# Two transformer blocks on one Trainium2 core: all tile arithmetic taken off GpSimd, three streams into one PSUM sum in the first block, the modulation GEMV at other places of the weight stream

## Chip, core and metric

The kernel runs on one core of a Trainium2 chip. The metric is the device time of one execution in microseconds (us). Engines are named as in the profile: PE (TensorE, matmuls), PEld (its weight loads), DVE (VectorE), ACT (ScalarE), POOL (GpSimd), SP (the queue that issues every DMA here).

## What is computed

One sequence of 256 tokens, width 2048, passes two different blocks, in float32. Cut to its products:

```python
h = rmsnorm(x, mix_norm_w)
u, qkv, z, b_raw, a_raw, g_s5, g_dn = split(h @ w_in)
y_s5 = gelu(s5_scan(u) + d * u)                        # complex diagonal state space
glu_a, glu_b = split(y_s5 @ s5_glu_w)
y_dn = deltanet(silu(causal_conv4(qkv)), z, b_raw, a_raw)   # 8 heads, chunked delta rule
merged = sigmoid(g_s5) * (glu_a * sigmoid(glu_b)) + sigmoid(g_dn) * (y_dn @ dn_proj_w)
x = x + merged @ w_out
act, val = split(causal_conv3(rmsnorm(x, ffn_norm_w) @ ffn_up))
x = rmsnorm(x + (silu(act) * val) @ ffn_down, final_norm_w)
# block 2
sh1, sc1, g1, sh2, sc2, g2 = split(silu(c) @ w_mod + b_mod)     # the GEMV, 2048 x 12288
h = rmsnorm(x) * (1 + sc1) + sh1
y = merge(window_attention(h @ w_in_2), gated_linear_attention(h @ w_in_2)) @ w_out_2
x = x + g1 * rmsnorm(y)
h = rmsnorm(x) * (1 + sc2) + sh2
x = x + g2 * rmsnorm((silu(gate) * val) @ w_down_2),  gate, val = split(causal_conv3(h @ w_up_2) + b)
```

## The kernel before

**The weight stream.** All weights, some 600 MB, pass once through the core. They are cut into jobs, one for each product (`job_list`): block 1 has u, ba, q, k, v, z, gs, glu, gdn, dnp, wout, up1a, dw1a, up1b, dw1b; block 2 has qa, ka, va, gk, qb, kb, vb, og, ga, gb, wba, wbb, wout2, up2a, dw2a, up2b, dw2b. A job is a list of groups of 128-column tiles. A chunk of up to 1 MB is fetched by one DMA (`fetch`, three buffers `raw`). `split` cuts a unit of 1024 columns of it into a high part `hi` (ACT, L413, a cast to fp32r) and the rest `lo` = raw - hi (L271, on DVE, or on POOL for the units that `on_pool` names). Activations are kept in the same two parts, 256 columns each, side by side in 512 columns.

**The product** (`run`). In form F, for every tile of k and every column tile, the loaded weights `hi` meet the 512 columns of both activation parts, and `lo` meets the 256 columns of the high part:

```python
T.matmul(cur[:, f, :], hi[:, s], x, start=first, stop=False)                    # L451
T.matmul(cur[:, f, 0:L], lo[:, s], x[:, 0:L], start=False, stop=last)           # L452
```

So one half of the PSUM bank holds hi*hi + lo*hi and the other hi*lo; `halves` adds them (an ACT copy, L469, and a DVE addition, L271, into a tile `ev`). In form T (wout, dw, va, vb: L457 to L459) the weights are what streams, and three matmuls of the same width go into one sum. Below, "a step" is one pair of tiles: a pair of matmuls in form F, three in form T.

**Evacuations** (`ev_u`, `ev_qkv`, `ev_z`, `ev_gate`, `ev_glu`, `ev_dnp`, `ev_up` and those of block 2) are generators, moved one yield at each few steps. In block 1 most multiply `ev` by the token scale `R` on POOL. `ev_gate` turns tanh into a gate on POOL and spills it to DRAM, whence `ev_glu` and `ev_dnp` load it.

**Beside the stream** run two background generators in block 1: `s5_task` (in eight rounds of `tables`, products, scans; `cmul` once ahead) and, after it, `dn_task`; in block 2 `attention_task` and `gla_task`. Their POOL operations go through `tt` (L271) and `ts` (L275) with the engine as the last argument. The sums of squares for the first norm are made on POOL from x.

**The GEMV.** `plan` puts 96 chunks of `w_mod` into the stream, one 1 MB transfer each, by the table `MOD_EVERY` (every second or third chunk of the jobs named). `split` multiplies and sums each on DVE (L404). `modulation` reads the results: 32 of the 96 at the start of block 2, the last 48 at its FFN.

What sets the order: each engine works its queue in order; the Tile scheduler makes the queues from the program order. Everything, transfers included, is issued by SP in one queue.

Of the kernel before, what the change touches and what calls it, by code (L numbers as in the profile page):

```python
# [256 lines left out]
class Kern:  # L257
# [131 lines left out]
    def on_pool(self, u):
        """Whether GpSimd makes the low parts of a unit."""  # L390
        j = self.chunks[self.units[u][0]][0].name
        n = u - self.job_start[j]
        e = self.POOL_EVERY.get(j, 0)
        return j in ("qa", "up2a") and n < 4 or e and n % e == 1
# [1507 lines left out]
```

## Time and profile before

| what | value |
|---|---|
| device time, median of 3 runs | 3260.02 us (3258.59 to 3263.13) |
| span of the profiled execution, first to last instruction | 3257.4 us |
| PE busy, share of the span | 3099.1 us, 95% |
| DVE busy | 2300.3 us, 71% |
| ACT busy | 1589.3 us, 49% |
| POOL busy | 872.4 us, 27% |
| HBM traffic over the span | 214 GB/s |
| mean granted PE clock | 0.985 |

The profiled execution's own time is known by its span alone; the median of the runs lies 2.6 us above that. Matmuls overlap in the records, so PE counts as busy even where it has slack; how densely it is fed is seen by the distance from one matmul to the next, or by the number of matmuls in a stretch.

### The profile page before, as it was taken

To read this page: it belongs to the slowest core of one execution; us is meant where nothing else is said; L and a number is where in the kernel's file an instruction comes from. 1 tells how busy PE (TensorE), PEld (TensorE's weight loads), DVE (VectorE), ACT (ScalarE), POOL (GpSimd) and SP (SyncE) were. 2 spreads that over 40 slices of the span, in tenths; PEclk is the share of its full clock that TensorE was granted. 3 is DMA by queue.
4 is the path that set the end of the run, shared out by engine and by line. 5 is a ranking of instruction groups with operands and counts; after the bars stand their busy time and mean duration, and the time that the engine had idled before them with its cause. 6 is when DMAs were issued, how large, how long until landed. Compare 5 with 4: busy or idle time off the path is not lost.

```text
span 3257.4 us, 46596 instructions
## 1 busy us (share of the span) xinstructions
PE 3099.1 (95%) x18220; PEld 2665.1 (82%) x18220; DVE 2300.3 (71%) x3043; ACT 1589.3 (49%) x2276; POOL 872.4 (27%) x491
## 2 busy tenths in 40 slices
PE   7889999999988999989989999999997999999998
PEld 6767789888877788777878898778887888898887
DVE  8999775666777767777667767887566666456655
ACT  4445543554444434444444544645444655445543
POOL 3665452231355403554020000332211111001101
PEclk9999999999999999999999999999998999999999
DMA  6334464665566677666756668666755555555553
GB/s 242 132 127 141 174 227 156 237 235 207 220 240 244 236 264 263 254 245 241 256 188 241 228 247 317 240 248 247 278 194 184 206 192 184 187 198 186 190 192 131
DMA packets 130829, 701.73 MB, mean 215 GB/s; under 512 B 20200, under 2 KB 33176, under 8 KB 53680
## 3 DMA queue, kind: packets, MB, share of 16 engines
q1 hardware_dynamic: 130608, 698.75, 60.0%
q8 instruction: 143, 2.34, 0.3%
q14 instruction: 78, 0.64, 0.1%
HBM read 674.26 MB, written 24.44 MB: 214 GB/s over the span
## 4 chain that ended last, share of the span: by engine, by line
PE 44%; DVE 3%; DMA 1%; issue 1%; ACT 1%; DVEq 0%; SPq 0%; ACTq 0%
PE main L451 19%; PE main L452 10%; PE main L457 5%; PE main L458 5%; PE main L459 5%; DMA raw<-in_wmod 1%; DVE lo L271 1%; DVE X L271 0%; PE bank L634 0%; DVE big L278 0%; ACT L282 0%; DVE raw L404 0%; DVE asm L275 0%; ACT X L282 0%; PE bank L1663 0%
## 5 line engine op out<-in xcount | busy, mean ns | idle before, releaser
L451 PE MATMUL main<-xs,hi 128*128 128x512 f32 x5440 | 1922.5, 396 | 17.2 <-ACT hi L413 9.2
L271 DVE TENSOR_TENSOR lo<-raw,hi 128x1024 fp32r<-128x1024 f32 x940 | 1201.3, 1282 | 628.7 <-ACT hi L413 626.1
L452 PE MATMUL main<-xs,lo 128*128 128x256 f32 x5440 | 1541.4, 284 | 56.4 <-DVE lo L271 38.7
L413 ACT CAST hi<-raw 128x1024 fp32r<-128x1024 f32 (+1 forms) x1024 | 1063.2, 1043 | 1000.7 <-PE main L451 560.5
L451 PEld LDWEIGHTS main<-xs,hi 128*128 128x128 f32 x5440 | 1030.5, 190 | 250.3 <-DVE xs L278 10.7
L452 PEld LDWEIGHTS main<-xs,lo 128*128 128x128 f32 x5440 | 1031.5, 190 | 83.6 <-DVE lo L271 49.8
L271 POOL TENSOR_TENSOR tmp<-tmp 128x256 f32<-128x256 f32 (+1 forms) x93 | 187.6, 2017 | 647.0 <-ACT tmp L282 646.6
L271 POOL TENSOR_TENSOR lo<-raw,hi 128x1024 fp32r<-128x1024 f32 x84 | 211.5, 2518 | 534.3 <-ACT hi L413 447.5
L404 DVE CUSTOM_DVE_ANT_0 raw<-raw,sc 128x2048 f32<-128x2048 f32 x96 | 242.4, 2525 | 42.2 <-DMA raw<-in_wmod 41.7
L271 POOL TENSOR_TENSOR ev<-ev,R 128x512 f32<-128x512 f32 x76 | 140.4, 1847 | 282.6 <-DVE ev L271 282.6
L278 DVE SCALAR_TENSOR_TENSOR tmp<-ev,pv,tmp 128x255 f32<-128x255 f32 (+1 forms) x352 | 162.7, 524 | 74.7 <-ACT tmp L282 74.7
L282 ACT ACTIVATE tmp<-ev,pv 128x256 f32<-128x256 f32 x176 | 88.1, 548 | 119.5 <-POOL ev L271 119.3
L271 DVE TENSOR_TENSOR ev<-main,evlo 128x512 f32<-128x512 f32 (+1 forms) x190 | 129.0, 679 | 14.3 <-ACT evlo L469 10.5
L457 PE MATMUL main<-hi,xs 128*128 128x256 f32 (+1 forms) x448 | 138.6, 309 | 0.0
L458 PE MATMUL main<-lo,xs 128*128 128x256 f32 (+1 forms) x448 | 137.4, 307 | 0.0
L459 PE MATMUL main<-hi,xs 128*128 128x256 f32 (+1 forms) x448 | 137.1, 306 | 0.0
L469 ACT COPY evlo<-main 128x512 f32<-128x512 f32 (+1 forms) x203 | 117.0, 576 | 13.7 <-PE main L452 13.7
L271 POOL TENSOR_TENSOR ev<-ev,tmp 128x512 f32<-128x512 f32 (+1 forms) x48 | 59.4, 1238 | 200.1 <-DVE ev L271 107.0
L451 PE MATMUL main<-ysp,hi 128*128 128x512 f32 x256 | 92.0, 400 | 0.4 <-DVE ev L271 0.4
L457 PEld LDWEIGHTS main<-hi,xs 128*128 128x128 f32 x448 | 84.1, 188 | 6.0 <-issue 1.7
L458 PEld LDWEIGHTS main<-lo,xs 128*128 128x128 f32 x448 | 84.3, 188 | 4.9 <-issue 0.7
L459 PEld LDWEIGHTS main<-hi,xs 128*128 128x128 f32 x448 | 84.5, 189 | 4.7
(336 smaller groups left out, 3863.0 us busy)
## 6 DMA issues: line engine op xcount, KB each, us to landing
raw<-in_w_in SPq DMA_DIRECT2D x164, 1024.0 KB, 4.9
raw<-in_wmod SPq DMA_DIRECT2D x96, 1024.0 KB, 5.1
raw<-in_ffn_up SPq DMA_DIRECT2D x88, 1024.0 KB, 5.0
raw<-in_w_up SPq DMA_DIRECT2D x88, 1024.0 KB, 4.8
raw<-in_ffn_down SPq DMA_DIRECT2D x38, 1024.0 KB, 5.0
raw<-in_w_down SPq DMA_DIRECT2D x38, 1024.0 KB, 4.8
raw<-in_w_out SPq DMA_DIRECT2D x32, 1024.0 KB, 4.8
raw<-in_s_glu_w SPq DMA_DIRECT2D x16, 1024.0 KB, 4.9
```

Of the source, the lines that this page charges most:

```text
L271: (eng or self.V).tensor_tensor(out=out, in0=a, in1=b, op=op)
L278: self.V.scalar_tensor_tensor(out=out, in0=a, scalar=s, in1=b, op0=op0, op1=op1)
L282: self.S.activation(out, a, f, bias=bias, scale=scale, **kw)
L404: self.V.tensor_tensor_reduce(r, r, self.sc, 1.0, 0.0, A.mult, A.add, self.mod[:, m:m + 1])
L413: self.S.copy(hi, r)
L451: T.matmul(cur[:, f, :], hi[:, s], x, start=first, stop=False)
L452: T.matmul(cur[:, f, 0:L], lo[:, s], x[:, 0:L], start=False, stop=last)
L457: T.matmul(cur[:, h, :w], xh, hi[:, s], start=first, stop=False)
L458: T.matmul(cur[:, h, :w], xh, lo[:, s], start=False, stop=False)
L459: T.matmul(cur[:, h, :w], xl, hi[:, s], start=False, stop=last)
L469: self.S.copy(lo[:, :nf], ps[:, :nf, L:])
```

## The change

- **One sum** (`ONE_SUM`, `run`): in the form F jobs of block 1, from u to dnp, and up1a, up1b, the pair of matmuls becomes three of 256 columns into one 256-column sum.
- **Evacuation straight out of PSUM** (`normed`): for these jobs one DVE product of PSUM and `R` stands for copy, addition and POOL product. `ev_glu` and `ev_dnp` read PSUM in a `scalar_tensor_tensor`; the +1 of the gates is folded into it, in block 2 too, and the gates' POOL step is gone.
- **No tile arithmetic on POOL**: `on_pool` is removed (all `lo` on DVE), and the POOL operations of the S5, DeltaNet, attention, GLA, FFN and norm code become DVE operations of the same size. The squares of the first norm are made by ACT from a second copy of x (`xt`, 2 MB, a new transfer at the start) in the buffer `ysp`.
- **The GEMV moved**: 34 of its 96 transfers leave up1a and up1b (20 and 22 there, now 4 and 4) for wout (5), dw1a and dw1b (8 each, now 12), gb (6, now 8), wba (4), wbb (8) and wout2 (7). `modulation` for the FFN of block 2 is read after wout2.
- Comments and docstrings are removed.

```diff
-    MOD_EVERY = {"up1a": 2, "dw1a": 3, "up1b": 2, "dw1b": 3, "qb": 2, "kb": 2, "vb": 2, "og": 2, "ga": 2, "gb": 2, "wba": 2, "wbb": 2}
+    MOD_EVERY = {"wout": 2, "up1a": 11, "dw1a": 2, "up1b": 11, "dw1b": 2, "qb": 2, "kb": 2, "vb": 2, "og": 2, "ga": 2, "gb": 2, "wba": 2, "wbb": 2, "wout2": 2}
...
-                if (ci >= 4 or nm != "up1a") and mods < 96 and since >= self.MOD_EVERY.get(nm, 1 << 30):
+                if (ci >= 6 or nm != "wout") and mods < 96 and since >= self.MOD_EVERY.get(nm, 1 << 30):
...
-    POOL_EVERY = {"gs": 4, "glu": 4, "ga": 4, "gb": 4, "up1a": 4, "up1b": 4}
...
-            eng = self.G if self.on_pool(u) else self.V
-            self.tt(lo, r, hi.bitcast(F32), A.subtract, eng)
+            self.tt(lo, r, hi.bitcast(F32), A.subtract)
...
+    ONE_SUM = ("u", "ba", "q", "k", "v", "z", "gs", "glu", "gdn", "dnp", "up1a", "up1b")
...
+                            if name in self.ONE_SUM:
+                                T.matmul(cur[:, f, 0:L], hi[:, s], x[:, 0:L], start=first, stop=False)
+                                T.matmul(cur[:, f, 0:L], hi[:, s], x[:, L:], start=False, stop=False)
+                                T.matmul(cur[:, f, 0:L], lo[:, s], x[:, 0:L], start=False, stop=last)
+                                continue
...
+    def normed(self, ps, nf=2):
+
+        out = self.sbt([P, 2, L], F32, "ev", 3, "ev")
+        self.tt(out[:, :nf], ps[:, :nf, :L], self.rbc(nf), A.mult)
+        return out
...
-        for i in range(4):
-            self.tt(sq[:, i > 0], x[:, 4 * i:4 * i + 4], x[:, 4 * i:4 * i + 4], A.mult, G)
...
+        xt = self.ys32.rearrange("p (h n) -> p h n", h=2)
+        self.dma(xt, ap["xt"])
+        for h in range(2):
+            self.act(self.tmp[:, 0:2048], xt[:, h], AF.Square, accum=self.ss[0][:, h, 0:1])
...
     def ev_qkv(self, t, ps):
-        raw = self.halves(ps)
-        yield
-        self.tt(raw, raw, self.rbc(2), A.mult, self.G)
-        yield
+        raw = self.normed(ps)
         yield
...
-            self.tt(o, x, p, A.mult, G)
+            self.tt(o, x, p, A.mult)
             self.tt(t3, y, q, A.mult)
...
-            self.roundn(r, e, eng=G)
-            self.tt(e, e, r, A.subtract, G)
-            yield
+            self.roundn(r, e)
+            self.tt(e, e, r, A.subtract)
...
-            self.tt(t1, t1, t2, A.add, G)
-            self.tt(t3, t3, t4, A.subtract, G)
+            self.tt(t1, t1, t2, A.add)
+            self.tt(t3, t3, t4, A.subtract)
...
     def ev_up(self, b, f, i, act, done, ps):
-        raw = self.halves(ps)
-        yield
-        if b == "1":
-            self.tt(raw, raw, self.rbc(2), A.mult, self.G)
-            yield
-            yield
+        raw = self.normed(ps) if b == "1" else self.halves(ps)
+        yield
...
-        self.tt(cv[:, 0], cv[:, 0], cv[:, 1], A.mult, self.G)
+        self.tt(cv[:, 0], cv[:, 0], cv[:, 1], A.mult)
...
-                if h and i in (1, 2):
-                    self.ts(y, y, r1[:, 1:2], A.mult, 0.0, A.add, G)
-                    self.tt(x, x, y, A.add, G)
-                else:
-                    self.stt(x, y, r1[:, h:h + 1], x, A.mult, A.add)
+                self.stt(x, y, r1[:, h:h + 1], x, A.mult, A.add)
...
     def ev_wbb(self, g, ps):
...
-        self.tt(raw, raw, t[:, 0], A.mult, self.G)
-        yield
-        self.tt(self.merged[:, 2 * g:2 * g + 2], raw, t[:, 1], A.add, self.G)
+        self.stt(raw, t[:, 0], 1.0, raw, A.add, A.mult)
+        yield
+        self.tt(self.merged[:, 2 * g:2 * g + 2], raw, t[:, 1], A.add)
```

Where the change moves instructions, three places of the queues show it. First SP at the very start, before and then with the change (`c_71` is a table of constants, `small`, `ysp` and `tmp` take what the S5 task loads):

```order
L285 DMA c_71<-in_c 128x272 [waits DMAHW3_49]
L285 DMA small<-in_s5p 128x96 [waits DMAHW4_49]
L285 DMA ysp<-in_s5c 128x2048 [waits DMAHW5_49]
L285 DMA raw<-in_w_in 128x2048 [waits DMAHW6_49,DVE_49]
L285 DMA raw<-in_w_in 128x2048 [waits DMAHW7_49,DMAHW0_49,DVE_49]
```

```order
L285 DMA c_71<-in_c 128x272 [waits DMAHW3_49]
L285 DMA ysp<-in_xt 128x4096 [waits DMAHW4_49]
L285 DMA small<-in_s5p 128x96 [waits DMAHW5_49]
L285 DMA raw<-in_w_in 128x2048 [waits DMAHW6_49,DVE_49]
L285 DMA raw<-in_w_in 128x2048 [waits DMAHW7_49,DMAHW0_49,DVE_49]
L285 DMA raw<-in_w_in 128x2048 [waits DMAHW2_49,DVE_49]
L285 DMA ysp<-in_s5c 128x2048 [waits DMAHW4_49,DMAHW1_49,Activation_49]
```

The 2 MB of `xt` come ahead of the fourth weight chunk, and the S5 loads now wait for ACT, which squares `xt` in the same buffer.

Second DVE in a round of the S5 task, before and then with the change (`big` holds the task's tables and states, `bank_64` and `bank_65` its PSUM, `pc` a ramp):

```order
L275 TENSOR_SCALAR big<-pc,small 128x128 x4
L271 TENSOR_TENSOR lo<-raw,hi 128x1024
L271 TENSOR_TENSOR ev<-main,evlo 128x512
L271 TENSOR_TENSOR big<-bank_64,big 128x2x128 x2
L271 TENSOR_TENSOR lo<-raw,hi 128x1024
L271 TENSOR_TENSOR big<-bank_65,big 128x2x128 x2
```

```order
L275 TENSOR_SCALAR big<-pc,small 128x128 x4
L1015 SCALAR_TENSOR_TENSOR big<-small,big 128x128 x4
L278 SCALAR_TENSOR_TENSOR big<-ev,pv,big 128x253 x2
L271 TENSOR_TENSOR ev<-main,R 128x512
L271 TENSOR_TENSOR lo<-raw,hi 128x1024
L271 TENSOR_TENSOR big<-big 128x512
L275 TENSOR_SCALAR big<-big 128x512
L271 TENSOR_TENSOR lo<-raw,hi 128x1024
L278 SCALAR_TENSOR_TENSOR big<-big 128x512
```

The 512-wide roundings, differences and sums that stood on POOL now stand between the `lo` of the stream; the evacuation is one row, with `R`, as before.

Third SP in wbb, before and then with the change (`d_gb` and `d_m` are spilled gates and sums, loaded into `tmp`; the numbers are the tensors'):

```order
L285 DMA tmp<-d_m_13725 128x512
L285 DMA raw<-in_w_branch_gla 128x2048 x2
L285 DMA tmp<-d_gb 128x512
L285 DMA tmp<-d_m_13725 128x512
L285 DMA raw<-in_w_branch_gla 128x2048 x2
```

```order
L285 DMA raw<-in_w_branch_gla 128x2048 x2
L285 DMA raw<-in_wmod 128x2048
L285 DMA tmp<-d_gb 128x512
L285 DMA tmp<-d_m_16277 128x512
L285 DMA raw<-in_w_branch_gla 128x2048 x2
L285 DMA raw<-in_wmod 128x2048
L285 DMA tmp<-d_gb 128x512
```

A 1 MB transfer of the GEMV now follows every two of weights there.

## Rows read from the trace of the kernel before

**Rows 1.** The page: the span, and busy time of each engine.
```profile
span 3257.4 us, 46596 instructions
...
PE 3099.1 (95%) x18220; PEld 2665.1 (82%) x18220; DVE 2300.3 (71%) x3043; ACT 1589.3 (49%) x2276; POOL 872.4 (27%) x491
```

**Rows 2.** Windows: stretch, length, busy us (instructions), clock, DMA share, GB/s: gdn, va.
```profile
core 0: us, PE busy (x) PEld busy (x) DVE busy (x) ACT busy (x) POOL busy (x), PEclk, DMA share, GB/s
609.00:697.70 88.70, 88.70 (x514) 78.09 (x513) 48.99 (x49) 44.60 (x56) 17.17 (x16) 1.00 0.62 221
1715.20:1726.70 11.50, 11.50 (x98) 11.50 (x98) 7.62 (x7) 4.69 (x5) 0.00 (x0) 1.00 0.77 271
```

**Rows 3.** Windows again: u to z; gs and glu; up1a; up1b.
```profile
7.40:353.80 346.40, 308.81 (x2153) 247.42 (x2154) 323.55 (x566) 165.25 (x221) 183.32 (x93) 0.95 0.44 157
353.80:609.00 255.20, 246.43 (x1549) 214.60 (x1548) 175.83 (x260) 122.54 (x189) 94.49 (x74) 0.99 0.60 203
835.60:1113.60 278.00, 253.31 (x1418) 215.58 (x1417) 216.35 (x248) 130.22 (x194) 150.84 (x62) 1.00 0.65 242
1241.60:1513.30 271.70, 251.60 (x1410) 215.78 (x1409) 211.44 (x236) 129.89 (x188) 139.93 (x62) 0.99 0.69 251
```

**Rows 4.** Timeline at the start, DVE and POOL: start, us, what.
```profile
13.22 3.21 POOL L271 TENSOR_TENSOR tmp<-tmp 128x1024 f32<-128x1024 f32 x1
...
14.15 9.14 DVE L278 SCALAR_TENSOR_TENSOR xs<-big,pv,xs 128x256 fp32r<-128x256 f32 x4
...
30.01 1.66 DVE L278 SCALAR_TENSOR_TENSOR xs<-big,pv,xs 128x256 fp32r<-128x256 f32 x4
```

**Rows 5.** DVE groups by shape, 7.4 to 373 us: busy us, mean ns, idle before.
```profile
L271 DVE TENSOR_TENSOR lo<-raw,hi 128x1024 fp32r<-128x1024 f32 x87 | 120.7, 1394 | 15.8 <-ACT hi L413 15.7
...
L278 DVE SCALAR_TENSOR_TENSOR big<-ev,pv,big 128x255 f32<-128x255 f32 x24 | 25.9, 1111 | 0.4 <-ACT big L282 0.4
...
L271 DVE TENSOR_TENSOR big<-big 128x512 f32<-128x512 f32 x24 | 15.9, 672 | 0.0
...
L278 DVE SCALAR_TENSOR_TENSOR xs<-big,pv,xs 128x256 fp32r<-128x256 f32 x14 | 15.4, 1153 | 0.6 <-ACT xs L282 0.6
...
L271 DVE TENSOR_TENSOR tmp<-ysp,small 128x1024 f32<-128x1024 f32 x2 | 2.4, 1210 | 0.0
```

**Rows 6.** DVE groups by shape in up2b, 2875.1 to 3119.2 us.
```profile
L271 DVE TENSOR_TENSOR lo<-raw,hi 128x1024 fp32r<-128x1024 f32 x89 | 109.1, 1226 | 59.5 <-ACT hi L413 58.9
L278 DVE SCALAR_TENSOR_TENSOR tmp<-ev,pv,tmp 128x255 f32<-128x255 f32 x42 | 18.3, 477 | 0.0
```

**Rows 7.** POOL groups by shape over the whole span: the S5 rounds.
```profile
L271 POOL TENSOR_TENSOR big<-big 128x512 f32<-128x512 f32 x32 | 51.8, 1635 | 22.7 <-DVE big L271 21.8
...
L275 POOL TENSOR_SCALAR big<-big 128x512 f32<-128x512 f32 x16 | 40.6, 2537 | 36.4 <-DVE big L278 19.5 <-DVE big L275 16.3 <-ACT ev L282 0.7
```

**Rows 8.** Windows: up2a; og; ga and gb; wba; wbb.
```profile
2504.00:2751.60 247.60, 247.60 (x1431) 218.13 (x1430) 171.28 (x243) 146.32 (x214) 30.14 (x21) 1.00 0.55 194
1944.80:2033.60 88.80, 88.80 (x515) 78.19 (x514) 65.56 (x64) 41.22 (x47) 2.42 (x1) 1.00 0.83 309
2033.60:2259.30 225.70, 213.39 (x1218) 181.62 (x1217) 183.10 (x268) 126.41 (x197) 72.65 (x46) 0.98 0.67 236
2259.30:2304.60 45.30, 45.30 (x259) 39.33 (x258) 28.34 (x30) 21.66 (x27) 10.31 (x8) 1.00 0.88 331
2304.60:2393.40 88.80, 88.80 (x515) 78.20 (x514) 50.52 (x51) 42.09 (x54) 24.89 (x15) 1.00 0.71 242
```

**Rows 9.** DVE groups by shape: the GEMV's product in up1a, then in og.
```profile
L404 DVE CUSTOM_DVE_ANT_0 raw<-raw,sc 128x2048 f32<-128x2048 f32 x21 | 59.0, 2808 | 0.8 <-DMA raw<-in_wmod 0.4
...
L404 DVE CUSTOM_DVE_ANT_0 raw<-raw,sc 128x2048 f32<-128x2048 f32 x8 | 18.3, 2289 | 0.7 <-DMA raw<-in_wmod 0.6
```

**Rows 10.** Timeline after wout2: the same four small DVE rows twice.
```profile
2485.53 2.82 DVE L275 TENSOR_SCALAR sm<-sm 128x2 f32<-128x2 f32 x4
...
2498.20 0.64 DVE L275 TENSOR_SCALAR sm<-sm 128x2 f32<-128x2 f32 x4
```

**Rows 11.** PE groups by shape, 7.4 to 373 us: two matmuls of the S5 rounds.
```profile
L1053 PE MATMUL bank<-big,ysp 128*32 128x127 f32 x256 | 13.0, 290 | 11.8 <-DVE big L271 10.2 <-DVE big L278 1.5
...
L1056 PE MATMUL bank<-big,ysp 128*32 128x128 f32 x256 | 8.5, 273 | 0.0
```

More of the change, by code (lines that the diff above doesn't have):

```diff
@@ L385, in fetch @@
             self.dma_at += 1
-    POOL_EVERY = {"gs": 4, "glu": 4, "ga": 4, "gb": 4, "up1a": 4, "up1b": 4}
[L389 to L394, printed above, removed]
     def split(self, upto):
@@ L709, in block1 @@
         self.run("z", self.xrhs, self.ev_z)
-        self.run("gs", self.xrhs, lambda g, ps: self.ev_gate(self.d_gs, g, ps, 1.0))
+        self.run("gs", self.xrhs, lambda g, ps: self.ev_gate(self.d_gs, g, ps))
         while not self.s5_done:
@@ L714, in block1 @@
         self.run("glu", lambda k: self.ysp[:, k], self.ev_glu)
-        self.run("gdn", self.xrhs, lambda g, ps: self.ev_gate(self.d_gdn, g, ps, 2.0))
+        self.run("gdn", self.xrhs, lambda g, ps: self.ev_gate(self.d_gdn, g, ps))
         self.finish(mix, "dn")
@@ L784, in ev_z @@
     def ev_z(self, g, ps):
[L785 to L788 removed]
+        raw = self.normed(ps)
         yield
@@ L794, in ev_z, with ev_gate @@
         self.z_done += 1
-    def ev_gate(self, dst, g, ps, c):
-        raw = self.halves(ps)
-        yield
-        self.tt(raw, raw, self.rbc(2), A.mult, self.G)
-        yield
+    def ev_gate(self, dst, g, ps):
+        raw = self.normed(ps)
         yield
         self.act(raw, raw, AF.Tanh, scale=0.5)
-        yield
-        self.ts(raw, raw, c, A.mult, c, A.add, self.G)
-        yield
         yield
@@ L811, in ev_glu @@
         self.dma(gl, self.d_gs[f // 2][:, L * (f % 2):L * (f % 2) + L])
-        raw = self.halves(ps)
+        raw = self.sbt([P, 2, L], F32, "ev", 3, "ev")
+        self.act(raw[:, 1], ps[:, 1, :L], AF.Tanh, scale=0.5)
         yield
-        self.act(raw[:, 1], raw[:, 1], AF.Tanh, scale=0.5)
+        self.stt(raw[:, 0], raw[:, 1], 1.0, ps[:, 0, :L], A.add, A.mult)
         yield
-        self.stt(raw[:, 0], raw[:, 1], 1.0, raw[:, 0], A.add, A.mult)
-        yield
-        self.tt(raw[:, 0], raw[:, 0], gl, A.mult, self.G)
+        self.stt(raw[:, 0], gl, 1.0, raw[:, 0], A.add, A.mult)
         yield
@@ L833, in ev_dnp @@
         t = self.ml.pop(g)
-        raw = self.halves(ps)
+        raw = self.sbt([P, 2, L], F32, "ev", 3, "ev")
+        self.stt(raw, t[:, 0], 1.0, ps[:, :, :L], A.add, A.mult)
         yield
-        self.tt(raw, raw, t[:, 0], A.mult, self.G)
-        yield
-        self.tt(raw, raw, t[:, 1], A.add, self.G)
-        yield
+        self.stt(raw, raw, 2.0, t[:, 1], A.mult, A.add)
         yield
@@ L1164, in dn_task @@
             ends = lambda t: t.rearrange("p (b n) -> p b n", n=P)[:, 0:3:2]
-            self.tt(k[:, h], k[:, h], r[:, 768:1024], A.mult, G)
-            self.tt(q[:, h], q[:, h], r[:, 1024:1280], A.mult, G)
-            self.tt(ends(at), ends(r[:, 0:384]), tri.unsqueeze(1).to_broadcast([P, 2, P]), A.add, G)
+            self.tt(k[:, h], k[:, h], r[:, 768:1024], A.mult)
+            self.tt(q[:, h], q[:, h], r[:, 1024:1280], A.mult)
+            self.tt(ends(at), ends(r[:, 0:384]), tri.unsqueeze(1).to_broadcast([P, 2, P]), A.add)
             yield
@@ L1374, in ev_down @@
                 self.square_sums(y, self.ss[1][:, :, g], True)
-            self.tt(x, x, row, A.mult, self.G)
+            self.tt(x, x, row, A.mult)
             if not last:
-                yield
                 yield
@@ L1380, in ev_down @@
         else:
-            self.tt(x, x, row, A.mult, self.G)
+            self.tt(x, x, row, A.mult)
     def shift_split(self, x, r, a, sh):
@@ L1444, in residual @@
                     x = self.x[:, h, c:c + 512]
-                    self.ts(x, x, sm[:, 4 + h:5 + h], A.mult, 0.0, A.add, G)
+                    self.ts(x, x, sm[:, 4 + h:5 + h], A.mult)
                     self.dma(d_x[:, h, c:c + 512], x)
@@ L1502, in block2 @@
         self.x = X.rearrange("p (h n) -> p h n", h=2)
+        self.run("wout2", self.xrhs, self.ev_wout2)
+        self.flush()
         sh2, sc2 = self.modulation(3), self.modulation(4)
@@ L1505, in block2 @@
         self.stt(a2, sc2, 1.0, self.pv("ffnpre", 0, 16), A.add, A.mult)
-        self.run("wout2", self.xrhs, self.ev_wout2)
-        self.flush()
         r1, r2 = sm[:, 4:6], sm[:, 6:8]
@@ L1532, in block2 @@
                 x, o = self.x[:, h, c], x2[:, h, c]
-                if h and i < 2:
-                    self.act(x, x, AF.Copy, scale=r1[:, 1:2])
-                    self.tt(o, o, x, A.add, G)
-                else:
-                    self.stt(o, x, r1[:, h:h + 1], o, A.mult, A.add)
+                self.stt(o, x, r1[:, h:h + 1], o, A.mult, A.add)
                 self.dma(ap["out"][:, h, c], o)
@@ L1574, in ev_gate2 @@
         yield
-        self.ts(raw, raw, 1.0, A.mult, 1.0, A.add, self.G)
-        yield
-        yield
         self.dma(dst[g], raw)
@@ L1604, in ev_wbb @@
         yield
-        self.tt(raw, raw, t[:, 0], A.mult, self.G)
+        self.stt(raw, t[:, 0], 1.0, raw, A.add, A.mult)
         yield
-        self.tt(self.merged[:, 2 * g:2 * g + 2], raw, t[:, 1], A.add, self.G)
+        self.tt(self.merged[:, 2 * g:2 * g + 2], raw, t[:, 1], A.add)
     def ev_wout2(self, g, ps):
@@ L1823, in gla_task @@
                 yield
-            self.tt(sq[0], sq[0], sq[1], A.add, G)
+            self.tt(sq[0], sq[0], sq[1], A.add)
             yield
             yield
-            self.tt(sq[0][:, 0:L], sq[0][:, 0:L], sq[0][:, L:], A.add, G)
+            self.tt(sq[0][:, 0:L], sq[0][:, 0:L], sq[0][:, L:], A.add)
             yield
```

48 lines of the change are left out of this document (16 added, 32 removed).

## The prediction

> **What bounds the kernel now.** I read the page first, then windows cut at the jobs (the main matmuls stand in the order of the job list, so each job's first one can be counted off), then the DVE rows by shape. The page [rows 1] says 95% for PE, but overlapping records hide slack; what counts is time per step. In gdn, 256 steps take 88.7 us with no gap: 346.5 ns for a pair of 512 and 256 columns, both weight loads inside it [rows 2]. A job at that pace is bound by PE. At it run gdn, og, wbb, up2b and nearly up2a [rows 2, 8]. The others are slower, and that is where time can be had:
>
> - u to z: 656 steps, 227 us at PE's pace, take 346.4 us. DVE is busy for 323.6 of them, 93% [rows 3]. This stage is bound by DVE, and POOL is the reason for part of it: four small DVE products took 9.14 us while POOL worked, and the same four 1.66 us once it had stopped [rows 4].
> - gs and glu: 255.2 us for 512 steps (177 us), DVE 175.8, the rest DeltaNet's own matmuls and chains [rows 3].
> - up1a and up1b: 704 steps each, 244 us at PE's pace, take 278.0 and 271.7 us, with DVE at 78% and POOL at over half [rows 3]. up2a, the same products without GEMV and with little on POOL, takes 247.6 [rows 8].
>
> **The change, part by part**, against the span of 3257.4 us; the median of the runs is 2.6 us above it.
>
> *Three streams for two.* 2960 steps turn from a pair into a triple of 256 columns. Form T shows that triple already: va has 32 of them in 11.50 us, 359 ns [rows 2]. So 13 ns more each, 38 us if all lay open. Only where PE sets the pace does it count by itself: gdn, dnp and ba, 400 steps, **+5 us**; elsewhere it is in the stage's own sum below. The Trainium skill ("TensorE: Matmul & The Clock Gate", section "Back-to-back issue gap") gives 262 cycles for 256 columns and 518 for 512, so a triple would cost 6 cycles more than a pair, 2.5 ns at 2.4 GHz, an estimate from that page. By it the term would be +1 us; the row is the closer witness, and I go by the row.
>
> *Evacuation.* A DVE addition of 512 becomes a DVE product of 512: nothing on DVE. ACT loses the copy, POOL its product; neither bounds a stage, and the shorter chain only brings PSUM free sooner. Nothing is counted.
>
> *u to z.* DVE loses its wait for POOL and gains POOL's work. The loss: `lo` ran at 1394 ns here and at 1226 in up2b, where POOL is nearly idle, 87 times, 15 us; the 255-wide convolution row at 1111 against 477, 24 times, 15 us; the `xs` products at 1153 against 415 (a quarter of 1.66), 14 times, 10 us [rows 4 to 6]. That is 40 us in 125 of the stage's 566 rows; the others mix short and long ones in the same way. Bounds 40 and 100; I take 75. The gain: 32 POOL rows of 512 at DVE's 672 ns, 21.5 us; 16 roundings of 512, which DVE never does here, between 0.2 and 0.67 us, taken at 0.45, 7 us; 12 products of `cmul` and a negation at 1210 ns, 16 us [rows 5, 7]. Together 44. DVE's time becomes 323.6 - 75 + 44 = 293, and with the 23 us in which it idled before, the stage takes 316 us: **-31**. PE needs 236 us there for its triples, so DVE stays the bound. The start's new transfer, 2 MB, is 6 us of DMA at wba's 331 GB/s and 9 at gdn's 221 [rows 2, 8], while three chunks of weights (16 steps, 5.8 us each) lie ahead of PE. It is covered; if that cover is thin, PE waits some 3 us inside the 316.
>
> *gs and glu.* PE +7 (512 steps). DVE gets 16 `lo` at 1226 ns and 24 products of 256, some 30 us, into 79 us of idle time, and loses waits for POOL (94 us of POOL in this stretch). Bounds -15 and +15, taken **+3**.
>
> *up1a and up1b.* Sixteen and eighteen GEMV rows leave each (2808 ns, [rows 9]), 45 us or more of DVE; 22 `lo` and 22 products of 256 (415 ns, [rows 4]) come, 36 us. DVE then has some 207 of 256 us, so PE binds: 704 triples are 253 us, and 3 more as in up2a over its pairs. 278.0 and 271.7 become 256 each: **-38**. Bounds -43 and -25.
>
> *The GEMV's 34 transfers elsewhere.* og carries 8 in 16 chunks at 88.8 us and loses nothing [rows 8]; its DVE row there is 2289 ns. wout, dw1a, dw1b and gb have that room: +2. wba already draws 331 GB/s at a DMA share of 0.88, which makes 376 GB/s full; with 4 MB more it would need 51 us for 45.3, so up to +6. wbb goes from 242 to about 337 GB/s, and DVE there from 50.5 to some 80 of 88.8 us: up to +6. I take **+9** in all; bounds 0 and 78 (34 times 2289 ns, all of it open).
>
> *Hand-overs.* After dw1b, after wout2 and at the end, DVE works alone while PE waits. Four tiny rows took 2.82 us beside a POOL `lo`, 0.64 without [rows 10]; the products that POOL shared come back to DVE at 0.67 each. **-7**, bounds 0 and -12.
>
> *ga and gb.* 512 steps are 177 us, the stage takes 225.7 with DVE at 81% and POOL at 32% [rows 8]. The GLA chain keeps its length, the long DVE rows go: **-10**, bounds 0 and -25.
>
> Sum: +5 - 31 + 3 - 38 + 9 - 7 - 10 = -69. Span 3188.4, median about **3191 us**.
>
> **The rivals.**
>
> *DVE's long rows are its own* (slower). If a row of 1394 ns stays so without POOL, DVE in u to z gains 44 us and loses nothing: 390 us instead of 346. gs and glu give +10, gdn to ba +5, the GEMV +9, up1 keeps its -38 since DVE still fits, the hand-overs and ga nothing: +30, 3290 us. Against it: the 1.66 beside the 9.14 [rows 4]. It decides where less than about a third of the difference between the two sums vanishes. The Trainium skill ("Perfetto Trace Analysis", section "Optimizing Scalar/DVE Operations") names offloading to GpSimd as worth a try when DVE is saturated, and doubts it in the same breath because the two share a port. Its first half would speak for this rival, its doubt for my forecast. Chance 6%.
>
> *PE becomes the bound of u to z.* The triples need 236 us; the other 841 matmuls, by two groups of S5 products (512 rows in 21.5 us, [rows 11]), some 35; with 10 us until x is there, 281 instead of 316: 3156 us. It needs DVE to lose 100 rather than 75 and its idle time too. Chance 14%.
>
> *The GEMV lies open.* If half of the 34 products hold up the `lo` behind them on DVE, 39 us instead of 9: 3221 us; if all do, 3260, no change. og speaks against it; wba's and wbb's loads and spills beside the stream for it. Chance 8%.
>
> *The third weight load is not hidden.* The Trainium skill ("TensorE: Matmul & The Clock Gate", section "The mechanism") says that a weight load overlaps a running matmul only in another row group. In the rows, PEld is busy for 78.1 of gdn's 88.7 us beside PE, 152 ns a load [rows 2]; 2960 of them in the open would be 450 us, 3640 in all. By that rule pairs could not run at 346 ns either; the trace does not agree. Chance 1%.
>
> *The change leaves work on POOL.* POOL's queue shrinks from 359 rows to 15, memsets and two tiny copies among them; excluded.
>
> **How the numbers follow.** My forecast has 71%. The unknown terms around it, u to z (-56 to +4), gs and glu, ga, GEMV, give 3150 to 3240; the range is 3145 to 3245, which takes in the PE rival and half of the GEMV one. Run medians scatter by under 0.2% (6.5 us), which I take as no change. Faster: the forecast, the PE rival and half or more of the GEMV rival, less a rest for errors that add up, 0.88. Within 0.2%: the GEMV rival in full, 0.05. Slower 0.07.
>
> **What would show it.** In the profile after, right: gdn at 92 us for 256 steps; `lo` at 1.23 us throughout with no DVE row of a small shape above 1 us; u to z at about 316 us with DVE over 90% busy; up1a and up1b at 256 us each, alike; og unchanged at 88.8. Wrong: gdn above 95 us (the triple costs more than in form T), `lo` above 1.3 us (the long rows are DVE's own), wba above 52 or wbb above 96 us with waits for w_mod transfers, or u to z near 346 with DVE below 85% (then chains, not DVE's load, set that stage).

## The result, and the profile after

The changed kernel takes 3143.45 us (median of 4 runs, 3137.57 to 3148.40) against 3259.56 for the kernel before in the same comparison: ratio 0.9639, 95% interval 0.9625 to 0.9653. It is 116 us faster where 69 were forecast. The time lies just under the low end of the range (3145).

The page of the changed kernel: span, busy time of each engine, and three groups (busy us, mean ns, idle before). They answer to [rows 1, 5, 6, 9].

```profile
span 3142.7 us, 51839 instructions
...
PE 3083.4 (98%) x21176; PEld 2804.5 (89%) x21176; DVE 2258.2 (72%) x3374; ACT 1540.9 (49%) x2170; POOL 3.0 (0%) x11
...
L271 DVE TENSOR_TENSOR lo<-raw,hi 128x1024 fp32r<-128x1024 f32 (+1 forms) x1024 | 1245.5, 1219 | 695.0 <-ACT hi L404 688.2
...
L395 DVE CUSTOM_DVE_ANT_0 raw<-raw,sc 128x2048 f32<-128x2048 f32 x96 | 219.6, 2288 | 47.9 <-DMA raw<-in_wmod 47.6
L278 DVE SCALAR_TENSOR_TENSOR tmp<-ev,pv,tmp 128x255 f32<-128x255 f32 (+1 forms) x352 | 146.6, 477 | 0.0
```

`lo` takes 1219 ns on average although all 1024 now run on DVE, and DVE, which took over all of POOL's arithmetic, is busy for 42 us less than before. The 255-wide row of the convolutions takes 477 ns on average; that of u to z, 1111 ns in [rows 5], takes 477 too.

Windows of the changed kernel, cut at its own jobs: u to z; gs and glu; gdn; up1a; up1b; ga and gb; wba; wbb. They answer to [rows 2, 3, 8].

```profile
core 0: us, PE busy (x) PEld busy (x) DVE busy (x) ACT busy (x) POOL busy (x), PEclk, DMA share, GB/s
7.60:288.00 280.40, 276.35 (x2520) 262.64 (x2521) 257.89 (x555) 144.81 (x184) 1.26 (x3) 0.99 0.56 201
288.00:561.50 273.50, 271.38 (x2345) 252.49 (x2344) 201.49 (x372) 119.45 (x181) 0.44 (x2) 1.00 0.57 190
561.50:651.60 90.10, 90.10 (x771) 90.10 (x770) 47.13 (x49) 42.97 (x50) 0.00 (x0) 1.00 0.63 219
789.70:1041.20 251.50, 251.50 (x2123) 251.50 (x2122) 185.42 (x266) 124.86 (x179) 0.00 (x0) 1.00 0.58 206
1164.30:1415.00 250.70, 250.70 (x2115) 250.70 (x2115) 183.27 (x249) 123.09 (x172) 0.00 (x0) 1.00 0.59 208
1927.70:2139.60 211.90, 208.55 (x1214) 179.75 (x1213) 174.42 (x287) 126.36 (x194) 0.00 (x0) 0.99 0.75 268
2139.60:2186.00 46.40, 45.50 (x263) 39.56 (x261) 37.19 (x60) 20.62 (x29) 0.00 (x0) 1.00 0.96 362
2186.00:2283.10 97.10, 92.81 (x512) 80.81 (x513) 77.35 (x86) 43.79 (x56) 0.00 (x0) 0.96 0.88 330
```

u to z fell from 346.4 to 280.4 us, while gs and glu rose from 255.2 to 273.5. up1a and up1b are alike now. og stays at 88.8. wbb rose from 88.8 to 97.1: the GEMV's transfers between them make its weights late. The first row of the waits of the changed kernel in wbb (engine and line waited for: us, times, longest):

```profile
ACT hi L404 <- DMA raw<-in_w_branch_gla: 25.1, 12, 5.6
```

### The profile page after: what moved, and what is told of

Same layout as the page of the kernel before. It is cut to its first block, busy times and chain, and to the rows that moved or that the text cites. A ratio compares the mean times of both kernels' runs of the same rounds, so it can differ in the third digit from the quotient of the medians.

```text
span 3142.7 us, 51839 instructions
## 1 busy us (share of the span) xinstructions
PE 3083.4 (98%) x21176; PEld 2804.5 (89%) x21176; DVE 2258.2 (72%) x3374; ACT 1540.9 (49%) x2170; POOL 3.0 (0%) x11
## 4 chain that ended last, share of the span: by engine, by line
PE 92%; DMA 3%; DVE 3%; ACT 1%; issue 1%; SPq 0%; DVEq 0%; ACTq 0%
PE main L448 20%; PE main L444 11%; PE main L446 11%; PE main L445 11%; PE main L449 10%; PE main L454 8%; PE main L455 8%; PE main L456 8%; DVE lo L271 1%; DMA tmp<-d_row 1%; PE bank L997 1%; DMA raw<-in_wmod 1%; DMA raw<-in_w_in 0%; DMA ysp<-in_xt 0%; DMA raw<-in_w_branch_gla 0%
## 5 line engine op out<-in xcount | busy, mean ns | idle before, releaser
L271 DVE TENSOR_TENSOR lo<-raw,hi 128x1024 fp32r<-128x1024 f32 (+1 forms) x1024 | 1245.5, 1219 | 695.0 <-ACT hi L404 688.2
L448 PE MATMUL main<-xs,hi 128*128 128x512 f32 x2864 | 1006.4, 395 | 4.2 <-ACT hi L404 3.3
L444 PE MATMUL main<-xs,hi 128*128 128x256 f32 x2576 | 728.3, 283 | 10.4 <-ACT hi L404 9.2
L445 PE MATMUL main<-xs,hi 128*128 128x256 f32 x2576 | 725.6, 282 | 0.0
L448 PEld LDWEIGHTS main<-xs,hi 128*128 128x128 f32 x2864 | 540.2, 189 | 127.3 <-ACT hi L404 4.5
L444 PEld LDWEIGHTS main<-xs,hi 128*128 128x128 f32 x2576 | 487.4, 189 | 15.7 <-ACT hi L404 9.6
L445 PEld LDWEIGHTS main<-xs,hi 128*128 128x128 f32 x2576 | 487.4, 189 | 2.1 <-issue 1.6
L395 DVE CUSTOM_DVE_ANT_0 raw<-raw,sc 128x2048 f32<-128x2048 f32 x96 | 219.6, 2288 | 47.9 <-DMA raw<-in_wmod 47.6
L278 DVE SCALAR_TENSOR_TENSOR tmp<-ev,pv,tmp 128x255 f32<-128x255 f32 (+1 forms) x352 | 146.6, 477 | 0.0
L454 PE MATMUL main<-hi,xs 128*128 128x256 f32 (+1 forms) x448 | 138.6, 309 | 0.0
L456 PE MATMUL main<-hi,act2a 128*128 128x512 f32 (+1 forms) x220 | 76.9, 349 | 0.0
```

Source lines behind the costliest of these rows:

```text
L271: (eng or self.V).tensor_tensor(out=out, in0=a, in1=b, op=op)
L278: self.V.scalar_tensor_tensor(out=out, in0=a, scalar=s, in1=b, op0=op0, op1=op1)
L395: self.V.tensor_tensor_reduce(r, r, self.sc, 1.0, 0.0, A.mult, A.add, self.mod[:, m:m + 1])
L444: T.matmul(cur[:, f, 0:L], hi[:, s], x[:, 0:L], start=first, stop=False)
L445: T.matmul(cur[:, f, 0:L], hi[:, s], x[:, L:], start=False, stop=False)
L454: T.matmul(cur[:, h, :w], xh, hi[:, s], start=first, stop=False)
```

## The experiments

Stage times, from the profiled run of each kernel, from one job's first main matmul to the next's (us). The last column is the median device time.

| kernel | u to z | gs to dnp | up1a + up1b | dw1a + dw1b | ga + gb | wba + wbb | time |
|---|---|---|---|---|---|---|---|
| before | 346.4 | 389.2 | 549.8 | 269.7 | 225.7 | 134.1 | 3259.6 |
| after | 280.4 | 409.0 | 502.0 | 258.3 | 211.9 | 143.5 | 3143.5 |
| e1, all on DVE only | 258.3 | 425.6 | 489.0 | 258.9 | 210.0 | 134.5 | 3118.5 |
| e2, GEMV moved only | 346.9 | 393.3 | 501.6 | 265.5 | 226.9 | 145.3 | 3217.9 |
| e3, after with pairs | 262.3 | 411.6 | 489.0 | 258.9 | 212.8 | 140.7 | 3113.9 |
| e4, after, GEMV back | 280.8 | 408.6 | 502.0 | 258.6 | 214.8 | 134.5 | 3136.9 |
| e5, e3 and e4 | 262.3 | 412.8 | 489.0 | 258.9 | 209.3 | 134.5 | 3104.6 |
| e6, tasks on POOL | 315.1 | 387.7 | 489.0 | 258.9 | 210.4 | 134.5 | 3138.7 |
| e7, `lo` on POOL | 258.5 | 423.2 | 507.4 | 260.1 | 218.1 | 134.1 | 3140.7 |
| e8, evacuations on POOL | 273.2 | 416.8 | 539.3 | 266.3 | 209.4 | 134.5 | 3179.5 |
| e12, shadow of e8 in up1 | 256.9 | 426.9 | 509.8 | 258.8 | 210.9 | 134.5 | 3138.0 |
| e13, e5, one sum in gs to dnp | 261.1 | 421.6 | 489.0 | 258.9 | 214.4 | 134.5 | 3118.4 |

### The parts of the change, one at a time

**e1: the kernel before, POOL's arithmetic on DVE, nothing else.**

```diff
-        (eng or self.V).tensor_tensor(out=out, in0=a, in1=b, op=op)
+        self.V.tensor_tensor(out=out, in0=a, in1=b, op=op)
...
-        (eng or self.V).tensor_scalar(out=out, in0=a, scalar1=s1, scalar2=s2, op0=op0, **kw)
+        self.V.tensor_scalar(out=out, in0=a, scalar1=s1, scalar2=s2, op0=op0, **kw)
...
-            eng = self.G if self.on_pool(u) else self.V
+            eng = self.V
```

> The kernel before with one thing changed: every tensor_tensor and tensor_scalar that POOL made is made by DVE. Pairs, copies out of PSUM and the places of the GEMV stay. Theory (the long DVE rows came from POOL, and they are most of the gain): the `lo` of 1024 columns falls to 1.22 us and no small DVE row stays above 1 us; u to z about 290 us (before 346.4, after the whole change 280.4), up1a and up1b about 258 each (before 278.0 and 271.8), ga 108; in all some 95 us of the 116 that the change gave, 3165 us (3145 to 3185). Rival (the one sum and the short evacuation, or the GEMV's new places, brought the gain; POOL's part is small): u to z stays above 325, up1a above 268, in all 3215 or more.

Measured: 3118.47 us, ratio 0.9569 (0.9547 to 0.9591). This part alone gives 141 us, more than the whole change and more than my range: u to z fell to 258 where I gave 290, up1a to 245 where I gave 258. Its windows, u to z and up1a:

```profile
7.00:265.20 258.20, 253.79 (x1680) 217.44 (x1681) 243.25 (x492) 137.88 (x183) 4.48 (x3) 1.00 0.58 208
...
783.50:1028.50 245.00, 245.00 (x1419) 215.75 (x1418) 225.44 (x315) 136.18 (x199) 0.00 (x0) 1.00 0.78 278
```

In u to z the 656 steps take 227 us at PE's pace, and the S5 task's own matmuls come on top: little of the 258 is left. But fewer of those matmuls stand there. The program of e1 differs from before in nothing but the engine of the arithmetic, yet PE has 1680 matmuls in u to z against 2153 [rows 3], with the 1312 of the weight stream in both; 473 others now stand behind the first matmul of gs. PE works its queue in order, so the queues themselves were made in another order. What that is worth beside the idle POOL was not separated. In up1a DVE carries the old GEMV and all of POOL's products in 225 of 245 us, and PE has no gap (704 steps at 348 ns).

**e2: the kernel before, only the GEMV's table (and the later reading) of the change.**

```diff
-    MOD_EVERY = {"up1a": 2, "dw1a": 3, "up1b": 2, ...
+    MOD_EVERY = {"wout": 2, "up1a": 11, "dw1a": 2, "up1b": 11, ...
```

> The kernel before with one thing changed: the GEMV's transfers at the places of the change (and the modulation read after wout2). POOL works as before. Theory (up1a and up1b were held by DVE's load, to which the GEMV and POOL's disturbance add; either gone is nearly enough): up1a and up1b fall to about 258 each (-34), wbb rises by 8 to 97, u to z and gs to dnp unchanged within 3; in all 3235 us (3222 to 3250). Rival (as my prediction had it in a term of its own: the GEMV only moves and costs 9 us elsewhere): up1a and up1b stay above 268, 3260 or more.

Measured: 3217.93 us, ratio 0.9874 (0.9854 to 0.9894); up1a 251.0 and up1b 250.6, wba and wbb 11.2 us more. The theory's direction held; the gain of 42 us was larger than it said, and the time lies below its range.

**e3: the changed kernel with pairs and two sums.** `ONE_SUM = ()`, and in `normed`, `ev_u`, `ev_ba`, `ev_glu` and `ev_dnp` the copy and the addition are back:

```diff
-        out = self.sbt([P, 2, L], F32, "ev", 3, "ev")
-        self.tt(out[:, :nf], ps[:, :nf, :L], self.rbc(nf), A.mult)
+        out = self.halves(ps, nf)
+        self.tt(out[:, :nf], out[:, :nf], self.rbc(nf), A.mult)
```

> The changed kernel with pairs instead of triples: two sums in PSUM, the ACT copy and the DVE addition back, then the product with R on DVE. Theory (a triple costs PE 5 ns more than a pair, and a pair costs DVE and ACT one more row in each evacuation; both small): gdn 88.8 (after 90.1), up1a and up1b 249 (after 251), u to z 280 to 290 as DVE gains 24 rows of 0.4 us; in all within 10 us of the changed kernel. Rival (the short evacuation is worth something of its own, as it frees PSUM sooner): 3160 us or more, with PE waiting for PSUM banks in u to z and gs.

Measured: 3113.92 us, ratio 0.9553 (0.9535 to 0.9570). My theory put the difference within 10 us and the rival made pairs slower; pairs are 29.5 us faster than the changed kernel. up1a gives the price of a triple:

```profile
774.00:1018.90 244.90, 244.90 (x1418) 215.73 (x1417) 197.07 (x286) 135.45 (x200) 0.00 (x0) 1.00 0.60 211
```

Against 251.50 after: 6.5 us over 704 steps, 9 ns a step, and 13 us for both halves. u to dnp take 673.9 us with pairs and 689.4 with triples, although DVE does more with pairs.

**e4: the changed kernel, the GEMV's table as before.**

> The changed kernel with the GEMV's transfers at their old places (20 and 22 in up1a and up1b). Theory (without POOL's disturbance DVE carries the GEMV in up1 beside PE: 185 us of rows and 16 more of 2.29 us are 222 of 251): up1a and up1b stay at 251 to 254, wbb falls back to 88.8, wba to 45.3; in all 3137 us (3130 to 3145), a little faster than the changed kernel, so the move gave nothing once POOL was idle. Rival (the move of the GEMV is what freed up1): up1a and up1b 265 or more each, in all 3165 or more.

Measured: 3136.86 us, ratio 0.9624 (0.9605 to 0.9644), as the theory said: up1a stays at 251.4 with 16 products more, wba and wbb lose their 9 us, ga and gb take 3 more. The same move that gained 42 us with POOL at work loses 6.6 without; the single runs of the two kernels overlap (3135.0 to 3141.4 and 3137.6 to 3148.4).

**e5: both undone, pairs and the old table.**

> The changed kernel with both of its other parts undone: pairs and two sums, and the GEMV at its old places. Theory (the one sum and the move each cost time, 30 and 7 us, and do not hang together): 3107 us (3101 to 3113), up1a and up1b 245 to 248 each, wbb 88.8. Rival (the old places of the GEMV fit only beside the one sum, as pairs bring back a DVE addition for each evacuation): 3115 or more, up1a and up1b above 250.

Measured: 3104.59 us, ratio 0.9530 (0.9516 to 0.9545). It is the fastest kernel here, 39 us below the changed one. Against e3 it gives the move once more, beside pairs: 9.3 us lost, and there no runs overlap.

e5 is also 13.9 us below e1, from which it differs in the small pieces of the change: the folded +1 of the gates, the first norm's squares on ACT, the later reading of the modulation. gs to dnp take 12.8 us less, u to z 4 more. These pieces stood in no term, and were not taken apart.

**e13: e5 with the one sum in gs, glu, gdn and dnp only.**

> The changed kernel with the GEMV at its old places and the one sum only in gs, glu, gdn and dnp; pairs in u to z, up1a and up1b. Theory (a triple costs PE 5 to 10 ns a step and gives nothing back where ACT and DVE have room): the 896 steps cost 4 to 5 us more than pairs, gs to dnp 413 to 418, in all 3104 to 3111 us, no faster than pairs throughout (3104.6). Rival (gs to gdn take 409 us with triples and 413 with pairs, because there the shorter evacuation counts): 3101 or less.

Measured: 3118.35 us, ratio 0.9564 (0.9550 to 0.9579). gs to dnp take 421.6 us against 412.8 in e5, more than I gave, and ga and gb, which the edit does not touch, 214.4 against 209.3; together these are the 13.8 us lost. The one sum does not pay in gs to dnp either. Why it costs 8.8 us there and not the triples' 4 to 5, and why ga and gb differ, is open.

**e10: the triple in another order** (`hi` high, `lo` high, `hi` low).

> The changed kernel with another order in the triple: hi on the high part, lo on the high part, hi on the low part. Theory (each of three matmuls of 256 columns takes 117 to 119 ns whatever it loads, so a triple costs 351 to 357 ns against 346.5 for a pair): gdn 90.1, up1a and up1b 251, in all 3143 us (3138 to 3149). Rival (loading the same weights twice running, or the turn of the moving data, sets the price): gdn nearer to 88.7 or above 91.5, up1a below 248 or above 254, in all 3135 or less, or 3152 or more.

Measured: 3143.44 us, the changed kernel's time; up1a falls from 251.4 to 248.7, gdn rises from 90.1 to 92.2, glu from 138.6 to 140.5, up1b stays at 250.6. So the order shifts a triple by a few ns either way and gains nothing in all; neither theory has it whole. Why a triple takes 352 ns in gdn and 357 in up1a, against 346.5 for a pair, is not settled.

### What POOL cost, and how

Each of the next three is e1 with one kind of work given back to POOL: in e6 the G of `s5_task` and `dn_task` is kept, in e7 `on_pool`, in e8 the `self.G` of the evacuations.

> The kernel before with all tile arithmetic on DVE but that of the S5 and DeltaNet tasks, which stays on POOL. Theory (POOL's rows lengthen DVE's, wherever they come from; the price shows where DVE is near its limit): u to dnp 715 us (before 735.6, with nothing on POOL 683.7), up1a and up1b 245, in all 3150 us (3130 to 3170). Rival (POOL relieves DVE of these rows in u to z, where DVE is busiest, and the two effects cancel): 3118 within 8.

> The kernel before with all tile arithmetic on DVE but the `lo` of the units that were POOL's (a quarter of those in gs, glu, up1a, up1b, ga, gb). Theory as for the tasks: POOL then has some 75 us in each of up1a and up1b; they rise from 245 to about 251 each, gs to gdn by 8, ga and gb by 4, u to z stays at 258; in all 3142 us (3124 to 3160). Rival (nobody is near a limit there, so the spared DVE rows and the lengthened ones both vanish): 3118 within 6.

> The kernel before with all tile arithmetic on DVE but that of the evacuations (the products with R, the gates, the products of the FFN and of the merges), which stays on POOL. Theory as for the tasks: u to dnp rises by about 20, up1a and up1b by 12 each, in all 3160 us (3135 to 3185). Rival (evacuations free PSUM before POOL begins, so nobody waits): 3118 within 8.

Measured: 3138.71, 3140.65 and 3179.46 us (ratios 0.9635, 0.9640 and 0.9758, intervals within 0.0016), 20, 22 and 61 us above e1. All three lie in the theory's ranges and none near its rival. Where they lie is not all as expected: in e6 u to dnp take 702.8 us instead of 715; in e7 up1a and up1b take 252.0 and 255.4, ga and gb rise by 8 instead of 4, and gs to dnp fall by 2 instead of rising; in e8 up1a and up1b rise by 25 each, twice what I gave them, and u to dnp by 6 instead of 20. The three prices add up to 103 of e1's 141 us; how the rest divides between POOL's other work (attention, GLA, the norms) and prices that do not simply add is not shown. e6 and e1 also differ in where the S5 task stands: with it on POOL, u to z take 57 us more and gs to dnp 38 less.

In e7 the POOL `lo` is slow and slows DVE's. Groups by shape in its up1a:

```profile
L271 DVE TENSOR_TENSOR lo<-raw,hi 128x1024 fp32r<-128x1024 f32 x66 | 90.9, 1386 | 1.3 <-ACT hi L413 1.3
L271 POOL TENSOR_TENSOR lo<-raw,hi 128x1024 fp32r<-128x1024 f32 x21 | 65.5, 3117 | 178.3 <-ACT hi L413 61.4 <-PE main L452 48.4 <-PE main L451 42.7
```

In e8 DVE's rows are hardly longer (`lo` takes 1269 ns in up1a, 1222 in e1), and yet up1a takes 270.4 us, 17.6 of them with PE idle until `lo` or `hi` was made. Groups by shape there:

```profile
L271 POOL TENSOR_TENSOR tmp<-tmp 128x256 f32<-128x256 f32 x20 | 69.9, 3493 | 53.9 <-ACT tmp L282 53.9
...
L282 ACT ACTIVATE tmp<-ev,pv 128x256 f32<-128x256 f32 x40 | 18.2, 502 | 53.0 <-POOL ev L271 53.0
...
L282 ACT ACTIVATE act1a<-tmp 128x256 fp32r<-128x256 f32 x20 | 8.4, 418 | 68.2 <-POOL tmp L271 68.2
```

POOL's product of 256 columns takes 3493 ns beside DVE's rows; DVE makes it in 416. ACT stands 121 us in all before the two rows that read POOL's products, and in its queue the casts to `hi` stand behind them:

```
L282 ACTIVATE tmp<-ev,pv 128x256 x2
L413 CAST hi<-raw 128x1024
L282 ACTIVATE tmp<-tmp 128x256
L282 ACTIVATE act1a<-tmp 128x256
L413 CAST hi<-raw 128x1024 x2
```

POOL's product lies between the third and the fourth of these, and ACT has nothing to do meanwhile. The kernel before has the same waits in its up1a:

```profile
ACT act1a L282 <- POOL tmp L271: 60.6, 20, 4.0
ACT tmp L282 <- POOL ev L271: 53.8, 19, 3.7
```

**e11: e8 with three more yields behind each of POOL's products in `ev_up`.**

> The kernel with only the evacuations on POOL (3179 us), and in the evacuation of up1a and up1b three more steps of the stream between POOL's product and the ACT operation that reads it, at both places. POOL does the same work. Theory (ACT, in order, stood 121 us in up1a before the rows that read POOL's products, and the casts to hi stood behind them): up1a and up1b fall from 270 and 269 to 250 or less, in all 3140 us (3132 to 3155). Rival (POOL's disturbance of DVE's rows is what cost the 25 us each): up1a and up1b stay above 262, in all 3168 or more.

Measured: 3184.43 us, ratio 0.9761 (0.9747 to 0.9776), no change. It did not test the theory: the scheduler left ACT's queue in up1a as it was, the same 195 rows in the same order. ACT's waits in e11 there:

```profile
ACT act1a L282 <- POOL tmp L271: 68.1, 19, 3.9
...
ACT tmp L282 <- POOL ev L271: 53.1, 19, 3.0
```

**e12: e1, and POOL repeats the two products of `ev_up` in block 1 from the same tiles into a scratch tile.**

```diff
             self.tt(raw, raw, self.rbc(2), A.mult, self.G)
+            self.G.tensor_tensor(out=self.dum[:, 0:2], in0=raw, in1=self.rbc(2), op=A.mult)
...
+            self.G.tensor_tensor(out=self.dum[:, 2], in0=cv[:, 0], in1=cv[:, 1], op=A.mult)
```

> The kernel before with all tile arithmetic on DVE (3118 us), to which POOL adds, in up1a and up1b, a copy of each product that it made there before (with R and of the two FFN halves), from the same tiles, at the same places, into a scratch tile that nobody reads. The order on ACT and DVE stays that of the kernel with nothing on POOL. Theory (up1a and up1b lost their 25 us to ACT and DVE standing in order before rows that read POOL's products, not to longer DVE rows): up1a and up1b 245 to 250, DVE's busy time in up1a up by 5 to 30 us (225 before), in all 3118 to 3130 us. Rival (POOL's rows, by lengthening DVE's, cost those 25 us): up1a and up1b 262 or more, 3150 or more.

Measured: 3138.03 us, ratio 0.9623 (0.9607 to 0.9639), between the two. up1a and up1b of e8, then of e12:

```profile
790.40:1060.80 270.40, 252.81 (x1418) 215.64 (x1417) 209.03 (x270) 130.32 (x195) 112.48 (x41) 1.00 0.68 248
1188.70:1457.60 268.90, 252.24 (x1410) 214.79 (x1409) 207.18 (x258) 128.38 (x188) 107.62 (x41) 1.00 0.70 254
```

```profile
783.80:1036.50 252.70, 248.30 (x1419) 215.69 (x1417) 248.77 (x311) 132.59 (x197) 100.32 (x41) 1.00 0.75 267
1160.00:1417.10 257.10, 248.51 (x1411) 214.84 (x1409) 251.00 (x298) 130.09 (x188) 95.63 (x40) 1.00 0.73 266
```

No engine waits for POOL in these two stages. POOL's rows lengthen DVE's by 23 us in up1a, DVE reaches the length of the stage, and the two stages lose 8 and 13 us. In e8 they lose 25 each with DVE at 209. So longer rows cost time where DVE is full. The rest of e8's loss, two thirds in up1a and half in up1b, is left to the waiting: e12's DVE carries the products as well, so its own loss should bound what the rows cost in e8. That is argued; no run took the waiting away and kept the work, as e11 was meant to.

**e9: e3, and POOL works on a scratch tile that nobody reads.**

> The changed kernel with pairs (3114 us), to which POOL work is added that nobody reads or waits for: one operation on a scratch tile of 512 columns with each unit of 1024 weights, a product in q and up1a, a memset in up1b, a copy in up2a, a tensor_scalar in up2b. Theory (POOL lengthens DVE's rows, but that costs time only where DVE has none to spare; what cost up1a and up1b 25 us each with the evacuations on POOL was the waiting in order behind POOL): q, where DVE is full, rises from 47 to 53 or more; DVE's busy time in up1a rises from 197 to 220 or more, yet up1a stays within 3 of 245; up1b, up2a and up2b (244.1, 246.7, 244.1) stay; in all 3121 us (3114 to 3132). Rival (the lengthened rows alone made up1a and up1b slow): up1a 260 or more, in all 3145 or more.

Measured: 3248.20 us, ratio 0.9956 (0.9941 to 0.9971). The work did not run in the jobs it was written for: it depends on nothing, and the queue let it start at once, kind after kind, from u to glu. So it says nothing of up1, and much of u to dnp, which rose from 673.9 to 806.8 us: 133 us lost to rows that nobody waits for (no engine's wait there ends with POOL). u to z of e9, where DVE is busy for 379 of 381 us:

```profile
7.90:388.60 380.70, 294.87 (x1748) 241.34 (x1749) 378.77 (x506) 143.37 (x190) 321.64 (x308) 0.89 0.40 143
```

And DVE's `lo` in three stretches of it: beside POOL's products (8 to 225.7 us), memsets (225.8 to 277.8) and copies (278 to 359.6), each with the POOL row.

```profile
L271 POOL TENSOR_TENSOR dum<-dum 128x512 f32<-128x512 f32 x100 | 169.5, 1695 | 7.7
L271 DVE TENSOR_TENSOR lo<-raw,hi 128x1024 fp32r<-128x1024 f32 x44 | 71.0, 1617 | 0.7 <-ACT hi L406 0.7
...
L415 POOL MEMSET dum<- 128x512 f32 x88 | 47.1, 535 | 5.1
L271 DVE TENSOR_TENSOR lo<-raw,hi 128x1024 fp32r<-128x1024 f32 x16 | 19.4, 1210 | 0.0
...
L417 POOL COPY dum<-dum 128x512 f32<-128x512 f32 x88 | 76.4, 868 | 5.4
L271 DVE TENSOR_TENSOR lo<-raw,hi 128x1024 fp32r<-128x1024 f32 x17 | 26.7, 1577 | 0.0
```

A POOL operation that only writes leaves `lo` at 1210 ns; one that reads a tile adds 367 on average, a product 407.

## Why the prediction was wrong

Direction and cause held: DVE's long rows came from POOL, and taking POOL's work back paid. The size failed. Term by term, in us, between the profiled spans (114.7 less in all; what the table lacks is 0.9 in small pieces):

| term | forecast | measured |
|---|---|---|
| gdn, dnp, ba: triples | +5 | +1.6 |
| u to z | -31 | -66 |
| gs and glu | +3 | +18 |
| up1a and up1b | -38 | -48 |
| GEMV elsewhere (wout, wba, wbb) | +9 | +9.5 |
| hand-overs (dw1b, wout2, dw2b) | -7 | -11 |
| ga and gb | -10 | -14 |
| dw1a, in no term | 0 | -5 |

- **The step that failed is DVE's time in u to z, 323.6 - 75 + 44 = 293 us, and with it "DVE stays the bound" at 316 us.** DVE was busy there for 257.9 us, and the stage took 280.4. The 75 holds: set each DVE row of before in u to z against the median of its line and shape where POOL stands idle, and add up: the excess is some 75 us. The time in which DVE idled holds too (22.5 us for 23). What did not come true is that the S5 task's rows stay in the stage. u to z hold 555 DVE rows where the 566 of before and the 61 that the sum adds make 627, and PE has 552 matmuls there beside the weight stream's where before had 841; gs and glu have 112 DVE rows more, 40 of them forecast, and gs rose from 111.6 to 134.9 us. The task is moved on by the steps of the stream, of which there are as many as before, so this is not an effect of the shorter time: as e1 shows, the queues were made in another order. DVE work thus went from a stage where DVE was full to one where it had room.
- **The rival's 281.** That 280.4 equals the sum of the rival in which PE becomes the bound is in part chance: it counted 841 other matmuls, and asked that DVE lose 100 us. That PE did come to set the pace is seen in who waits; ACT, which makes `hi`, waits for PE to use up the old ones:

```profile
ACT hi L404 <- PE main L445: 100.1, 57, 3.5
...
DVE lo L271 <- ACT hi L404: 13.7, 19, 1.8
```

- **u to dnp together.** The sum had to be made over all of them: forecast -23, measured -46. That is half of the 46 us missed. PE is idle for 6 of these 689 us.
- **up1.** I left the shared rows out of this stage's sum, and so had DVE at 207 us after; it is 185. That changed nothing in the time: PE bound, as forecast. The miss is the triple, taken at 13 ns over the pair from [rows 2] plus 3 us for the stage; it is 9 in up1 and 5.5 in gdn (90.1 less 88.7 over 256 steps). The Trainium skill ("TensorE: Matmul & The Clock Gate", "Back-to-back issue gap") gave 2.5 by the estimate from its table: nearer than mine in gdn, further off in up1, and too low in both.
- **Where the prediction read the change wrongly although its sum did not show it.** It gave the triples 5 us of their own, counted them beyond that only inside the sums of other stages, and took the GEMV's move as part of up1's gain. By e3 and e4 the one sum costs 29.5 us and the move 6.6 (9.3 beside pairs): two of the three parts lose, and the first, -141 by e1, pays for all. So part of the agreement is luck, as errors offset each other: without these losses the miss would have been larger (e5 is 154.5 us below before). "Only where PE sets the pace does it count" was right, but once POOL is idle PE sets the pace nearly everywhere.
- **The waits.** The prediction looked for POOL's price in longer rows. That ACT waited in order for POOL's products (121 us in up1a of e8) was not in any term; by the argument from e12 that is about half or more of e8's loss in up1. In the kernel before ACT waited for POOL's rows 114 us in up1a, and 45 in u to z. How much of before's loss there is of this kind was not separated.
- **wbb.** My sign for an error there was a time above 96 with waits for the `w_mod` transfers. It came to 97.1, but with waits of ACT for the weights' own transfers. The term of +9 holds: 8.4 in wbb, above its bound of 6, and 1.1 in wba.
- **Rivals.** Long rows of DVE's own: excluded by `lo` at 1219. GEMV in the open: the move costs 6.6 us by e4 and 9.3 by e5 against e3. The third weight load: a triple of three loads runs in 352 ns in gdn, so they are hidden. Work left on POOL: the pages count 491 instructions before and 11 after (3.0 us), where the prediction has 359 and 15.
- **A bound without a row.** No row stands behind the 0.2 us that the prediction gives as the least for a rounding of 512 on DVE; after the change the 16 roundings take 419 ns each, near the 0.45 taken.

## What to carry to other kernels

Price the parts of a change against each other, not each against the kernel before: with POOL at work the GEMV's move gained 42 us, without it the move lost 7, since each of the two had been enough to relieve DVE in up1. Once an engine is relieved, find the next bound first and see which other parts of the change spend just that: here the triples spent PE's time to save ACT's and DVE's, which had become free. Work that runs beside a stream has no fixed stage: another engine for it can change where the queues place it. Count it in the queues of the changed kernel, or sum over all the stages it may fall into.
